# Where the operands of 6500 matrix products lie in SBUF: from an offset of 64 bytes to one of 128

## The chip, the cores and the metric

The kernel runs on 1 core of one Trainium2 chip. The metric is the device time of one execution in microseconds, as the median of several runs. One execution was also taken by the hardware profiler; all durations below come from that one.

## The reference, cut to what matters

Two layers of a diffusion backbone over 512 latent tokens of width 1024 with 256 context tokens. Layer 0 is attention (four global heads and four windowed heads with a sink), layer 1 a Fourier mixer over four channel groups. Each layer ends with a gated feed-forward part with a depthwise convolution of width 3. Everything is float32.

```python
y, yc = attention_mixers(h, hc, attn_w_in[a], ...)      # layer 0
y = fourier_mix(h) @ w_f                                # layer 1
x = x + g1 * rms_norm(y, norm_g[i, 1])
h = modulate(rms_norm(x, norm_g[i, 2]), sh2, sc2)
x = x + g2 * rms_norm(conv_ffn(h, ffn_w_up[i], ffn_conv_w[i], ffn_conv_b[i], ffn_w_down[i]), norm_g[i, 3])

def conv_ffn(h, w_up, conv_w, conv_b, w_down):          # D_FF = 2816
    u = h @ w_up
    ...                                                 # width-3 convolution along the tokens
    gate, val = jnp.split(u, 2, axis=-1)
    return (jax.nn.silu(gate) * val) @ w_down
```

## The kernel before

Activations are held transposed: channels on the 128 partitions, tokens along the row. Every large matrix product is done in fp32r; each operand is split into a high part and a rest (`split`: ScalarE copies to the high part, VectorE or GpSimd subtracts), and each product becomes three (`mm3`, lines 104 to 106): high weights by high data, high by rest, rest by high. `PE.matmul(out, lhsT=weights, rhs=moving)` loads 128 columns of `lhsT` into TensorE and streams `rhs` (256 to 512 columns) past them. So a product reads two places of SBUF, and the load of the weights of the next product (PEld in the profile) goes on while the moving operand of the present one streams. In names such as `mm<-hh,wl` the first name after the arrow is the moving operand and the second the weights.

The order of work: the modulation vectors and norms of the inputs; projections to keys and values, to queries; attention by head, with the remaining projections filled in between; the output projection; feed-forward of layer 0; Fourier mixing; feed-forward of layer 1; the last norm and the store. Weights arrive by DMA in three rotating `raw` buffers and are split into five rotating pairs `wh`/`wl`. Some weights are kept in the pairs `xh`/`xl` and `zh`/`zl`, which at other times hold activations as moving operands. In parts of the feed-forward stages, seven products of 256 columns take the place of eight (`seven_products`).

Where a tile lies follows from its pool: tiles of a pool follow one another in the order in which their tags first appear, each rounded up to 32 bytes, and a pool begins where the one below it ends. In the kernel before, counting modulo 256 bytes: `hh`, `hl` and `xT` start at 0, `wh` and `wl` at 192, `th`/`tl`, `kh`/`kl`, `B`, `Z` at 128, `qh`/`ql` at 192; the buffers of `xh`/`xl` and of `zh`/`zl` are partly at 0 and partly at 128, since some are 4224 bytes long, and weights kept in them are moved on by `SIDE` = 16 elements of 4 bytes (`beside`), to 64 or 192. So in nearly every product the two operands differ by 64 or by 192 modulo 256 bytes. Offsets inside a tile (the chunk `k`, the token block) are multiples of 256 bytes, except for rows of 288 elements (`A`, `ct`), which step by 128.

Of the kernel before, what the change touches and what calls it, by code (L numbers as in the profile page):

```python
# [10 lines left out]
F32 = mybir.dt.float32  # L11
F32R = mybir.dt.float32r
# [7 lines left out]
P = 128  # L20
D = 1024
KC = D // P
T = 512
TT = T // P
# [25 lines left out]
GP = [1, 1]  # L50
BP = [4, 1]

SIDE = 16

WARM = 36
HOT = [5, 8, 5, 6]
# [18 lines left out]
C_C, C_CC, C_MB, C_NG, C_CW, C_CB = 0, 8, 16, 112, 176, 440  # L75
C_SINK, C_ALL = 528, 532

K_ID, K_SEL, K_QD, K_ALL = 0, 128, 256, 260
# [3 lines left out]
def kernel(ctx: ExitStack, tc: tile.TileContext, a):  # L82
    nc = tc.nc
    V, S, G, PE, SY = nc.vector, nc.scalar, nc.gpsimd, nc.tensor, nc.sync
    cnt = [0]
    nbufs = {}

    def mk(pool, shape, dt=F32, tag=None, bufs=1):
        cnt[0] += 1
        n = nbufs.setdefault((id(pool), tag), (pool, bufs))[1]  # L90
        return pool.tile(shape, dt, tag=tag, name=f"{tag}_{cnt[0]}", bufs=n)
# [8 lines left out]
    def f(ap):  # L100
        return ap.bitcast(F32)
# [24 lines left out]
    def split(h, l, src, eng=V):  # L126
        i = S.copy(out=h, in_=src), eng.tensor_tensor(out=l, in0=src, in1=f(h), op=ALU.subtract)  # L127
        for j in i:
            held(j)

    cp = ctx.enter_context(tc.tile_pool(name="cp", bufs=1))
    wp = ctx.enter_context(tc.tile_pool(name="wp", bufs=1))
# [4 lines left out]
        return t  # L137

    def wpair(shape):
        return mk(wp, shape, F32R, "wh", 5), mk(wp, shape, F32R, "wl", 5)  # L140

    away = mk(ctx.enter_context(tc.tile_pool(name="dr", bufs=1, space=bass.MemoryType.DRAM)), [P, KC, T], F32, "away")
    cols = mk(cp, [P, C_ALL], F32, "cols")
    SY.dma_start(out=cols[:, :C_CW], in_=a["cols"][:, :C_CW])
    con = mk(cp, [P, K_ALL], F32, "con")
    xT = mk(cp, [P, KC, T], F32, "xT")
    yT = mk(cp, [P, KC, T], F32, "yT")
    hh = mk(cp, [P, KC, T], F32R, "hh")
    hl = mk(cp, [P, KC, T], F32R, "hl")
    ident = con[:, K_ID:K_ID + P]  # L150
    ones32 = mk(cp, [P, 32], F32, "ones32")
    V.memset(ones32, 1.0)
    scol = mk(cp, [P, 2, KC], F32, "scol")
    eps = mk(cp, [P, 1], F32, "eps")
    once = mk(cp, [P, 1], F32, "once")
    mk(cp, [P, 8], F32, "cpad")
    V.memset(eps, EPS)
    mods = mk(cp, [P, 2, 6, KC], F32, "mods")
    der = mk(cp, [P, 2, 4, KC], F32, "der")
# [16 lines left out]
    W4 = HT // 4  # L176
# [12 lines left out]

    def rstd(ps):  # L190
        w = ps.shape[1]
        v, t, r = (mk(cp, [P, W4], F32, "st_" + c, n)[:, :w] for c, n in (("v", 2), ("t", 1), ("r", 2)))
        S.activation(out=r, in_=ps, func=AF.Abs_reciprocal_sqrt, bias=eps, scale=1.0 / D)
        V.tensor_scalar(out=v, in0=ps, scalar1=1.0 / D, scalar2=EPS, op0=ALU.mult, op1=ALU.add)
        V.tensor_tensor(out=t, in0=r, in1=r, op=ALU.mult)
        V.scalar_tensor_tensor(out=t, in0=t, scalar=-0.5, in1=v, op0=ALU.mult, op1=ALU.mult)
        V.scalar_tensor_tensor(out=v, in0=t, scalar=1.5, in1=r, op0=ALU.add, op1=ALU.mult)
        return v
# [361 lines left out]
    with ExitStack() as es:  # L560
# [27 lines left out]
        with ExitStack() as e1:  # L588
# [21 lines left out]
            def load_kva(c):  # L610
                kva[c] = raw([P, 2, T], a["w_kva"][c])
# [4 lines left out]

            load_x(0)
            load_mod(0)
            SY.dma_start(out=con, in_=a["con"])
            load_kva(0)  # L620
            load_mod(1)
            SY.dma_start(out=cols[:, C_CW:], in_=a["cols"][:, C_CW:])
# [118 lines left out]
            for s in START.split():  # L741
                n = [int(c) for c in s[1:]]
# [163 lines left out]
        with ExitStack() as e2:  # L906
            at = e2.enter_context(tc.tile_pool(name="at", bufs=1, reuse_waits="tile"))
# [28 lines left out]
            def pv(head, Ps, vh, vl):  # L936
                is_a = head < 4
                po = mk(aps, [P, T], F32, "O", 1)
                cs, th, tl = {}, {}, {}

                def turn(kt):
                    t = kt - 2
                    lo, hi = (0, 4) if is_a or kt < 2 else (max(0, t - 1), min(4, t + 2))
                    c = cs[kt] = slice(lo * P, hi * P)
                    pt = mk(aps, [P, T], F32, "PT", 2)
                    for j in range(lo, hi):
                        if is_a:
                            off = kt * P
                        else:
                            off = kt * P if kt < 2 else TC + (t - max(0, j - 1)) * P  # L950
                        PE.transpose(out=pt[:, j * P:(j + 1) * P], in_=Ps[j][:, off:off + P], identity=ident)  # L951
                    th[kt] = mk(at, [P, T], F32R, "th", 2)
                    tl[kt] = mk(at, [P, T], F32R, "tl", 2)
                    split(th[kt][:, c], tl[kt][:, c], pt[:, c])

                turn(0)
                turn(1)
                yield
                for kt in range(6):
                    c = cs[kt]  # L960
                    mm3(po[:, c], vh[:, kt, :], vl[:, kt, :], th[kt][:, c], tl[kt][:, c], kt == 0, kt == 5)
                    if kt < 4:
                        turn(kt + 2)
                    if kt < 5:
                        yield
                if head < KEPT:
                    S.copy(out=kept(head)[0], in_=po.rearrange("p (t d) -> p t d", d=P))
                else:
                    split(hh[:, head, :], hl[:, head, :], po)
                yield  # L970

            V.tensor_scalar(out=nsink, in0=cols[:, C_SINK:C_SINK + 4], scalar1=-1.0, scalar2=None, op0=ALU.mult)
            pend = iter(())

            def queries_t(head):
                qh = mk(at, [P, T], F32R, "qh", 1)
# [10 lines left out]
            for head in range(8):  # L987
# [6 lines left out]
                for j in range(TT):  # L994
# [4 lines left out]
                    if is_a:  # L999
                        for i in range(2):  # L1000
                            o = ps[:, 128 + i * 384:128 + (i + 1) * 384]
                            mm3(o, qh[:, qs], ql[:, qs], kh[:, i * 384:(i + 1) * 384],
                                kl[:, i * 384:(i + 1) * 384], True, True)
                        reg, n = ps[:, 128:896], NK
                    else:
# [4 lines left out]
                        o = ps[:, 512:512 + nl]  # L1010
# [7 lines left out]
                        reg, n = ps[:, 256:512 + nl], TC + nl  # L1018
# [30 lines left out]
                    i = 4 * (head - 6) + j  # L1049
# [41 lines left out]

    def beside(pool, shape, tag):
        n, m = shape[1:]
        return mk(pool, [P, 2 * SIDE + n * m], F32R, tag, 4)[:, SIDE:SIDE + n * m].rearrange("p (a b) -> p a b", b=m)

    class Pairs:
        def __init__(self, es):
# [14 lines left out]
            return [beside(self.first, shape, n) for n in ("xh", "xl")]  # L1112

        def spare_weights(self, shape):
            return [beside(self.pool, shape, n) for n in ("zh", "zl")]

    def up_weights(l, pairs, fis, eng=V):
        for fi in fis:
# [342 lines left out]
    with ExitStack() as es:  # L1461
        up = es.enter_context(tc.tile_pool(name="up", bufs=1, reuse_waits="tile", side="right"))
        M1 = 258
        B = [mk(up, [P, 4, 256], F32R, "B%d" % i) for i in range(2)]
        A = [mk(up, [P, 4, 288], F32R, "A%d" % i)[:, :, :M1] for i in range(2)]
        N = [mk(up, [4, M1 + 30], F32R, "N%d" % i)[:, :M1] for i in range(2)]
        mk(up, [P, 24], F32, "upad")
        wk = es.enter_context(tc.tile_pool(name="wk", bufs=1, reuse_waits="tile", side="right"))
        zs = ExitStack()
        zp = zs.enter_context(tc.tile_pool(name="zp", bufs=1, reuse_waits="tile"))  # L1470
        ft = wpair([P, 2, 256])
        st = wpair([P, TT, 256])
        Z = [mk(zp, [P, TT, 4, 256], F32R, "Z%d" % i) for i in range(2)]
        ct = [mk(zp, [P, 32 + TT * 288], F32R, "ct%d" % i)[:, SIDE:SIDE + TT * 288].rearrange(
            "p (t m) -> p t m", t=TT)[:, :, :M1] for i in range(2)]
        split(ft[0], ft[1], raw([P, 2, 256], a["dft_c"]), G)
        lc = raw([P, TT, M1], a["dft_lc"])
        ls = raw([P, TT, 256], a["dft_ls"])
# [2 lines left out]
        def over_channels(g, h):  # L1481
# [11 lines left out]
            if h:  # L1493
                split(Z[0][:, 2:4, g, :], Z[1][:, 2:4, g, :], ps)
                return
            for t in range(2):
                rc = r0[:, 2 * t:2 * t + 1]
                held(S.activation(out=Z[0][:, t, g, :], in_=ps[:, t, :], func=AF.Copy, scale=rc))
                held(V.scalar_tensor_tensor(out=Z[1][:, t, g, :], in0=ps[:, t, :], scalar=rc,
                                            in1=f(Z[0][:, t, g, :]), op0=ALU.mult, op1=ALU.subtract))  # L1500

# [53 lines left out]
        def group(g, ts):  # L1555
            cosines(g, [v[:, g, :] for v in A], [z[:, :, g, 0:P] for z in Z], ts, fb[:, g:g + 1])
            ps = over_tokens((g // 2,), g % 2, [z[:, :, g, P:] for z in Z], st, ts, g % 2 == 1)
            if ts[-1] == TT - 1 and g % 2:
# [51 lines left out]
        group(1, [2, 3])  # L1610
        cosines(None, N, [z[:, :, :, P] for z in Z], list(range(TT)), fb[:4, 4:5])
        group(3, [2, 3])
# [5 lines left out]
        for d in range(KC):  # L1618
            wh, wl = w_f.pop() if w_f else fourier_weights(d)
# [7 lines left out]
            pp = mk(pps, [P, T], F32, "mm", 6)  # L1627
            mm3(pp[:, :M1], nyh[:, d * P:(d + 1) * P], nyl[:, d * P:(d + 1) * P], N[0], N[1], True, False)
            for g in range(4):
                mm3(pp[:, :M1], wh[:, 0, g, :], wl[:, 0, g, :], A[0][:, g, :], A[1][:, g, :], False, g == 3)  # L1630
            qs = mk(wk, [P, 256], F32, "qs", 2)
# [14 lines left out]
    with ExitStack() as es:  # L1646
# [13 lines left out]
        for k in range(0, KC, 2):  # L1660
            t = mk(cp, [P, T], F32, "sq", 2).rearrange("p (a b) -> p a b", a=2)
# [97 lines left out]
```

## Time and profile before

| | |
|---|---|
| median of 3 runs | 1138.37 us (1137.33 to 1138.49) |
| the profiled execution | 1137.78 us |
| its span | 1136.0 us, 19565 instructions |
| mean granted clock of TensorE | 0.996 |
| HBM read, written | 148.28 MB, 6.29 MB |

In rows of groups, a line reads: source line, engine, operation, out<-in, rows by columns of the array in use, shape of the output, count, then busy us, mean ns of one, and idle time of the engine before it. Matmuls are pipelined: a product's duration reaches past the start of the next one, so durations overlap and their sum is more than the time. In rows for one tile or one line, three numbers with slashes are the smallest, the median and the largest duration in ns, and after them stand the first and the last start.

### The profile page before, as it was taken

How to read it: one execution, taken by the hardware profiler on the slowest of the kernel's cores; microseconds unless marked ns; L12 is line 12 of the kernel's file. 1: busy time of each engine (PE TensorE's matmuls, PEld its weight loads, DVE VectorE, ACT ScalarE, POOL GpSimd, SP SyncE). 2: the span in 40 equal slices, each digit the busy share in tenths (PEclk: the TensorE clock that was granted, in tenths of full speed). 3: DMA queues.
4: the chain of work that ended last, by engine and by line, in shares of the span. 5: the costliest groups of instructions: out<-in, count | busy, mean ns of one | idle time of the engine just before them, and what ended most of it. 6: DMA issues, size and time to landing. Idle time of an engine off the chain costs nothing.

```text
span 1136.0 us, 19565 instructions
## 1 busy us (share of the span) xinstructions
PE 1105.1 (97%) x7810; PEld 962.1 (85%) x7810; DVE 902.3 (79%) x1469; ACT 595.4 (52%) x1068; POOL 174.6 (15%) x180
## 2 busy tenths in 40 slices
PE   9999999999999999999999999999999999999995
PEld 5689888868888978987899898779888898999995
DVE  4678777765679976987999668978998998879755
ACT  4342356666666633552465445557746555555533
POOL 1136332421420000000000143620000000000012
PEclk9999999999999999999999999999999999999998
DMA  9676101075143355635535401742215533322342
GB/s 370 252 237 217 44 1 39 10 266 207 38 186 112 103 200 217 223 121 204 196 111 173 135 2 57 231 122 113 74 47 163 189 103 116 103 91 93 105 144 75
DMA packets 33763, 155.83 MB, mean 137 GB/s; under 512 B 3460, under 2 KB 8196, under 8 KB 22024
## 3 DMA queue, kind: packets, MB, share of 16 engines
q1 hardware_dynamic: 32520, 150.39, 37.5%
q0 software_dynamic: 1152, 4.19, 1.6%
q8 instruction: 61, 1.00, 0.4%
q14 instruction: 30, 0.25, 0.1%
HBM read 148.28 MB, written 6.29 MB: 136 GB/s over the span
## 4 chain that ended last, share of the span: by engine, by line
PE 77%; DVE 14%; ACT 5%; DMA 2%; issue 2%; POOL 1%; DVEq 0%; POOLq 0%; ACTq 0%; SPq 0%
PE mm L104 21%; PE mm L106 20%; PE mm L105 20%; DVE wl L127 2%; PE PT L951 1%; DMA raw<-in_w_up 1%; DVE md_t L305 1%; PE O L104 1%; PE O L105 1%; PE gm L530 1%; PE gm L104 1%; PE gm L106 1%; ACT wh L127 1%; PE gm L105 1%; PE O L106 1%
## 5 line engine op out<-in xcount | busy, mean ns | idle before, releaser
L127 ACT CAST wh<-raw 128x1024 fp32r<-128x1024 f32 (+2 forms) x207 | 190.6, 933 | 167.8 <-PE mm L105 115.4
L127 DVE TENSOR_TENSOR wl<-raw,wh 128x1024 fp32r<-128x1024 f32 (+2 forms) x197 | 214.7, 1098 | 52.2 <-ACT wh L127 51.9
L104 PE MATMUL mm<-hh,wh 128*128 128x256 f32 (+1 forms) x632 | 204.8, 325 | 1.9 <-ACT yT L926 0.9
L106 PE MATMUL mm<-hh,wl 128*128 128x256 f32 (+1 forms) x632 | 202.0, 320 | 0.4 <-DVE wl L127 0.2
L105 PE MATMUL mm<-hl,wh 128*128 128x256 f32 (+1 forms) x632 | 202.0, 320 | 0.0
L280 POOL TENSOR_TENSOR gacc<-gacc,sq 128x256 f32<-128x256 f32 (+1 forms) x33 | 28.0, 848 | 712.6 <-ACT sq L278 711.9
L104 PEld LDWEIGHTS mm<-hh,wh 128*128 128x128 f32 x632 | 118.7, 188 | 17.0 <-ACT sq L1206 4.6
L105 PEld LDWEIGHTS mm<-hl,wh 128*128 128x128 f32 x632 | 118.7, 188 | 10.3
L106 PEld LDWEIGHTS mm<-hh,wl 128*128 128x128 f32 x632 | 118.7, 188 | 10.2 <-DVE wl L127 1.2
L104 PE MATMUL mm<-zh,wh 128*128 128x256 f32 x384 | 109.5, 285 | 1.2 <-ACT sq L1209 0.6
L104 PE MATMUL mm<-xh,wh 128*128 128x512 f32 (+1 forms) x302 | 107.1, 355 | 0.0
L105 PE MATMUL mm<-zl,wh 128*128 128x256 f32 x384 | 107.1, 279 | 0.0
L106 PE MATMUL mm<-zh,wl 128*128 128x256 f32 x384 | 107.0, 279 | 0.0
L105 PE MATMUL mm<-xl,wh 128*128 128x512 f32 (+1 forms) x302 | 106.5, 353 | 0.0
L106 PE MATMUL mm<-xh,wl 128*128 128x512 f32 (+1 forms) x302 | 106.2, 352 | 0.0
L104 PEld LDWEIGHTS mm<-zh,wh 128*128 128x128 f32 x384 | 72.1, 188 | 5.5 <-ACT sq L1209 4.2
L106 PEld LDWEIGHTS mm<-zh,wl 128*128 128x128 f32 x384 | 72.5, 189 | 0.0
L105 PEld LDWEIGHTS mm<-zl,wh 128*128 128x128 f32 x384 | 72.1, 188 | 0.0
L104 PEld LDWEIGHTS mm<-xh,wh 128*128 128x128 f32 x302 | 56.7, 188 | 9.4 <-issue 1.6
L105 PEld LDWEIGHTS mm<-xl,wh 128*128 128x128 f32 x302 | 56.7, 188 | 8.5 <-issue 0.4
L106 PEld LDWEIGHTS mm<-xh,wl 128*128 128x128 f32 x302 | 56.8, 188 | 8.0
L1267 ACT ACTIVATE cv<-mm,cols 128x512 f32<-128x512 f32 x59 | 45.7, 776 | 23.1 <-PE mm L106 17.4
(435 smaller groups left out, 2796.1 us busy)
## 6 DMA issues: line engine op xcount, KB each, us to landing
raw<-in_w_up SPq DMA_DIRECT2D x42, 1024.0 KB, 4.9
xT<-in_mod_r SPq DMA_DIRECT2D x20, 1024.0 KB, 5.0
raw<-in_w_down SPq DMA_DIRECT2D x32, 384.0 KB, 3.1
raw<-in_mod_p SPq DMA_DIRECT2D x8, 1024.0 KB, 4.9
raw<-in_w_down SPq DMA_DIRECT2D x16, 512.0 KB, 3.9
raw<-in_w_in SPq DMA_DIRECT2D x6, 1024.0 KB, 8.2
yT<-in_mod_r SPq DMA_DIRECT2D x10, 512.0 KB, 7.3
raw<-in_w_out SPq DMA_DIRECT2D x4, 1024.0 KB, 5.1
```

Source lines behind the costliest of these rows:

```text
L104: i = PE.matmul(out, lhsT=ah, rhs=bh, start=start, stop=False, skip_group_check=skip)
L105: PE.matmul(out, lhsT=ah, rhs=bl, start=False, stop=False, skip_group_check=skip)
L106: return i, PE.matmul(out, lhsT=al, rhs=bh, start=False, stop=stop, skip_group_check=skip)
L127: i = S.copy(out=h, in_=src), eng.tensor_tensor(out=l, in0=src, in1=f(h), op=ALU.subtract)
L280: G.tensor_tensor(out=self.acc[:, sl], in0=self.acc[:, sl], in1=sq[:, sl], op=ALU.add)
L305: m = V.scalar_tensor_tensor(out=t, in0=yT[:, k, hs], scalar=der[:, l, gi, k:k + 1], in1=R, op0=ALU.mult, op1=ALU.mult)
L530: PE.matmul(ps[32 * q:32 * q + 32, :], lhsT=spad[:, k, :], rhs=w[:, q * T:(q + 1) * T], start=k == 0, stop=k == KC - 1)
L951: PE.transpose(out=pt[:, j * P:(j + 1) * P], in_=Ps[j][:, off:off + P], identity=ident)
L1267: S.activation(out=cv, in_=ps, func=AF.Identity, bias=bc, scale=wc[1])
```

## The change

The places of tiles are shifted with unused pieces, so that the moving operand of nearly every fp32r product starts at 0 modulo 256 bytes and its weights at 128, or the reverse. For that, `SIDE` becomes 32 elements, the buffers `xh`/`xl` get 1088 elements (4352 bytes, a multiple of 256) when they hold weights, `zh`/`zl` 1024, `A` and `ct` rows of 320 elements, and unused tiles stand ahead of `wh`, behind `wl`, and ahead of `qh`, `th`, `Z` and `ct` and behind `N`. To make room, `scol` takes the place of the columns of `cols` from which it is computed, `eps` and `once` become two more columns of `con`, and `st_r` has one buffer, not two.

```diff
-SIDE = 16
+SIDE = 32
+XW = 1088
+QPAD, TPAD, ZPAD, UPAD = 16, 48, 64, 56
+WPAD = 24
...
     def wpair(shape):
-        return mk(wp, shape, F32R, "wh", 5), mk(wp, shape, F32R, "wl", 5)
+        if (id(wp), "wh") in nbufs:
+            return mk(wp, shape, F32R, "wh", 5), mk(wp, shape, F32R, "wl", 5)
+        mk(wp, [P, WPAD], F32, "wpad")
+        w = mk(wp, shape, F32R, "wh", 5), mk(wp, shape, F32R, "wl", 5)
+        mk(wp, [P, 48], F32, "wpad2")
+        return w
...
-    con = mk(cp, [P, K_ALL], F32, "con")
+    con = mk(cp, [P, K_ALL + 2], F32, "con")
...
-    scol = mk(cp, [P, 2, KC], F32, "scol")
-    eps = mk(cp, [P, 1], F32, "eps")
-    once = mk(cp, [P, 1], F32, "once")
-    mk(cp, [P, 8], F32, "cpad")
+    scol = cols[:, C_C:C_C + 16].rearrange("p (a b) -> p a b", a=2)
+    eps = con[:, K_ALL:K_ALL + 1]
+    once = con[:, K_ALL + 1:K_ALL + 2]
...
-        v, t, r = (mk(cp, [P, W4], F32, "st_" + c, n)[:, :w] for c, n in (("v", 2), ("t", 1), ("r", 2)))
+        v, t, r = (mk(cp, [P, W4], F32, "st_" + c, n)[:, :w] for c, n in (("v", 2), ("t", 1), ("r", 1)))
...
-            SY.dma_start(out=con, in_=a["con"])
+            SY.dma_start(out=con[:, :K_ALL], in_=a["con"])
...
+                    if (id(at), "th") not in nbufs:
+                        mk(at, [P, TPAD], F32, "tpad")
                     th[kt] = mk(at, [P, T], F32R, "th", 2)
...
+            mk(at, [P, QPAD], F32, "qpad")
...
     def beside(pool, shape, tag):
         n, m = shape[1:]
-        return mk(pool, [P, 2 * SIDE + n * m], F32R, tag, 4)[:, SIDE:SIDE + n * m].rearrange("p (a b) -> p a b", b=m)
+        return mk(pool, [P, XW], F32R, tag, 4)[:, SIDE:SIDE + n * m].rearrange("p (a b) -> p a b", b=m)
...
         def spare_weights(self, shape):
-            return [beside(self.pool, shape, n) for n in ("zh", "zl")]
+            n, m = shape[1:]
+            o = SIDE if n * m + SIDE <= 1024 else 0
+            return [mk(self.pool, [P, 1024], F32R, t, 4)[:, o:o + n * m].rearrange("p (a b) -> p a b", b=m)
+                    for t in ("zh", "zl")]
...
-        A = [mk(up, [P, 4, 288], F32R, "A%d" % i)[:, :, :M1] for i in range(2)]
-        N = [mk(up, [4, M1 + 30], F32R, "N%d" % i)[:, :M1] for i in range(2)]
-        mk(up, [P, 24], F32, "upad")
+        A = [mk(up, [P, 4, 320], F32R, "A%d" % i)[:, :, :M1] for i in range(2)]
+        N = [mk(up, [4, 320], F32R, "N%d" % i)[:, :M1] for i in range(2)]
+        mk(up, [P, UPAD], F32, "upad")
...
+        mk(zp, [P, ZPAD], F32, "zpad")
         Z = [mk(zp, [P, TT, 4, 256], F32R, "Z%d" % i) for i in range(2)]
-        ct = [mk(zp, [P, 32 + TT * 288], F32R, "ct%d" % i)[:, SIDE:SIDE + TT * 288].rearrange(
-            "p (t m) -> p t m", t=TT)[:, :, :M1] for i in range(2)]
+        mk(zp, [P, 32], F32, "zpad2")
+        ct = [mk(zp, [P, TT, 320], F32R, "ct%d" % i)[:, :, :M1] for i in range(2)]
```

More of the change, by code (lines that the diff above doesn't have):

```diff
@@ L148 @@
     hh = mk(cp, [P, KC, T], F32R, "hh")
+    ident = con[:, K_ID:K_ID + P]
     hl = mk(cp, [P, KC, T], F32R, "hl")
-    ident = con[:, K_ID:K_ID + P]
     ones32 = mk(cp, [P, 32], F32, "ones32")
     V.memset(ones32, 1.0)
-    scol = mk(cp, [P, 2, KC], F32, "scol")
-    eps = mk(cp, [P, 1], F32, "eps")
-    once = mk(cp, [P, 1], F32, "once")
-    mk(cp, [P, 8], F32, "cpad")
+    scol = cols[:, C_C:C_C + 16].rearrange("p (a b) -> p a b", a=2)
+    eps = con[:, K_ALL:K_ALL + 1]
+    once = con[:, K_ALL + 1:K_ALL + 2]
     V.memset(eps, EPS)
```

## The prediction

> **What bounds the kernel now.** I read the page's totals first, then the chain that ended last, then the busy times by stage, and only then the products by shape.
>
> ```profile
> span 1136.0 us, 19565 instructions
> PE 1105.1 (97%) x7810; PEld 962.1 (85%) x7810; DVE 902.3 (79%) x1469; ACT 595.4 (52%) x1068; POOL 174.6 (15%) x180
> PEclk9999999999999999999999999999999999999998
> PE 77%; DVE 14%; ACT 5%; DMA 2%; issue 2%; POOL 1%; DVEq 0%; POOLq 0%; ACTq 0%; SPq 0%
> ```
>
> ```profile
> 340.00:680.00 340.00, 338.57 (x2108) 297.57 (x2107) 283.50 (x361) 166.97 (x255) 15.06 (x18) 1.00 0.43 150
> 770.00:1106.00 336.00, 333.70 (x2208) 298.38 (x2207) 287.11 (x420) 193.10 (x315) 4.29 (x6) 1.00 0.33 111
> ```
>
> TensorE is busy for 97% of the span and carries 77% of the chain. The second view has two stretches, most of the two feed-forward parts (length, then PE, PEld, DVE, ACT and POOL busy, granted clock, DMA). There TensorE is idle for 1.43 and 2.30 us out of 676, at a granted clock of 1.00, while VectorE, next in line, is busy for 83% and 85%. So in these stages a nanosecond per product goes straight into the time, and the question is one number: how long one fp32r product holds TensorE, and whether the place of its operands changes that.
>
> **Does place matter at all?** First groups by shape in two short windows (the last two columns are mean ns and idle time), then starts from the timeline of the same stage, then a 512-column run.
>
> ```profile
> L104 PE MATMUL mm<-zh,wh 128*128 128x256 f32 x2 | 0.6, 276 | 0.0
> ```
>
> ```profile
> L104 PE MATMUL mm<-zh,wh 128*128 128x256 f32 x3 | 0.8, 280 | 0.0
> L106 PE MATMUL mm<-zh,wl 128*128 128x256 f32 x3 | 0.8, 279 | 0.0
> ```
>
> ```profile
> 500.28 0.28 PE L104 MATMUL mm<-zh,wh 128*128 128x256 f32 x1
> 501.19 0.28 PE L106 MATMUL mm<-zh,wl 128*128 128x256 f32 x1
> 502.48 0.28 PE L104 MATMUL mm<-zh,wh 128*128 128x256 f32 x1
> 503.42 0.28 PE L106 MATMUL mm<-zh,wl 128*128 128x256 f32 x1
> ```
>
> ```profile
> L106 PE MATMUL mm<-hh,wl 128*128 128x512 f32 x7 | 2.8, 394 | 0.0
> L104 PE MATMUL mm<-hh,wh 128*128 128x512 f32 x6 | 2.3, 388 | 0.0
> ```
>
> The first row is from 500.7 to 501.1 us, the next two from 502.5 to 503.3. Helper, shape and weights pool are the same; the moving buffer differs. From the tile sizes in the code, wh and wl sit at 192 modulo 256 bytes. The zh buffer of the first window sits at 128 (moving minus weights: -64), that of the second at 0 (+64). Eight intervals between starts take 0.91 us in the first (114 ns each) and 0.94 in the second (118). That is the same 4 ns by which the durations differ, so a duration can be read as the interval plus a constant. The two signs of the 64-byte offset do not cost the same: quick is 276, slow is 280. With 512 columns, at +64, the products of a triple go from 388 to 394, though all have the same offset: place is not the only thing that sets the step.
>
> One row speaks against place:
>
> ```profile
> L106 PE MATMUL mm<-ct,Z 128*4 128x258 f32 x4 | 1.1, 282 | 0.0
> ```
>
> These products load 4 columns of weights, not 128, so that almost no weight load lies beside them, and with two columns more than 256 they still take 282 ns. The slow step exists without a rival stream.
>
> [...]
>
> **The change, part by part.** By adding up the tile sizes, afterwards hh, hl, xT, the gated pairs xh/xl, the blocks zh/zl, A, B, N, Z, th/tl, kh/kl and ch/cl start at 0 modulo 256, and wh/wl, ct, qh/ql and the weights kept in xh/xl at 128. No compute instruction and no transfer is added or removed. The effect is in the product rate, on these groups:
>
> ```profile
> L105 PE MATMUL mm<-hl,wh 128*128 128x256 f32 x400 | 112.1, 280 | 0.0
> L105 PE MATMUL mm<-zl,wh 128*128 128x256 f32 x384 | 107.1, 279 | 0.0
> L105 PE MATMUL mm<-hl,xh 128*128 128x256 f32 x128 | 36.3, 284 | 0.0
> L106 PE MATMUL mm<-xh,wl 128*128 128x256 f32 x112 | 31.3, 279 | 0.0
> L105 PE MATMUL mm<-wl,hh 128*128 128x256 f32 x112 | 31.4, 280 | 0.0
> L106 PE MATMUL gm<-wh,hl 128*128 128x256 f32 x96 | 26.9, 280 | 0.0
> L105 PE MATMUL mm<-xl,zh 128*128 128x256 f32 x84 | 23.5, 280 | 0.0
> L105 PE MATMUL mm<-hl,wh 128*128 128x512 f32 x224 | 87.6, 391 | 0.0
> L106 PE MATMUL mm<-hh,wl 128*128 128x512 f32 x224 | 88.0, 393 | 0.1
> L105 PE MATMUL mm<-xl,wh 128*128 128x512 f32 x190 | 74.7, 393 | 0.0
> L106 PE MATMUL mm<-xh,wl 128*128 128x512 f32 x190 | 74.9, 394 | 0.0
> L104 PE MATMUL mm<-xh,wh 128*128 128x512 f32 x190 | 75.4, 397 | 0.0
> L105 PE MATMUL mm<-xT,wh 128*128 128x512 f32 x64 | 25.0, 390 | 0.0
> ```
>
> ```profile
> L105 PE MATMUL mm<-hl,xh x160: 276/276/470, 277.2 to 789.7; 128*128 128x256 f32 x128, 128*128 128x258 f32 x32
> ```
>
> Each group runs on three lines (L104 to L106) with the same count; I take the line with the fewest waits. The mean of 284 for hl,xh holds waits; its median in the last row is 276.
>
> The good end: every product becomes quick. With 256 columns the excess over 276 is 4 ns x 400 + 3 x 384 + 0 x 128 + 3 x 112 + 4 x 112 + 4 x 96 + 4 x 84 = 4256 ns for one line, 12.8 us for three. With 512 columns, over 388, L105 gives 3 x 224 + 5 x 190 + 2 x 64 = 1750 ns, which I use for L104 too, and L106 gives 5 x 224 + 6 x 190 + 2 x 64 = 2388; together 5.9 us. Sum 18.7 us. The feed-forward stages hold 4316 products (2108 + 2208), against 3 x 1794 = 5382 in the list: about three quarters, where all of it counts. Of the last quarter, in stages where the chain passes through other engines, I count half: 18.7 x 0.875 = 16.4 us.
>
> The bad end: every product becomes slow. With 256 columns up to 280: (1 x 384 + 4 x 128 + 1 x 112) x 3 = 3.0 us. With 512 columns up to 397, the highest group mean here: L105 gives 6 x 224 + 4 x 190 + 7 x 64 = 2552 ns, taken twice, L106 4 x 224 + 3 x 190 + 7 x 64 = 1914; together 7.0 us. Sum 10.0 us, of which I let all count. A step beyond what is seen, 4 ns more on 3 x 1316 products of 256 columns, would add 15.8 us more; that is left to the tail.
>
> Where between the ends? No product of before runs steadily at 128. But now and then an odd one does, where the weights loaded during it belong to another kind of product. th (at 128) is followed in places by a product with weights from hh (at 0):
>
> ```profile
> L106 PE MATMUL O<-th,wl 128*128 128x512 f32 x32 | 12.6, 395 | 0.0
> ```
>
> ```profile
> L106 PE MATMUL O<-th,wl x1: 390/390/390, 158.5 to 158.5; 128*128 128x512 f32 x1
> L106 PE MATMUL O<-th,wl x1: 390/390/390, 188.1 to 188.1; 128*128 128x512 f32 x1
> L104 PE MATMUL O<-th,wh x1: 397/397/397, 162.9 to 162.9; 128*128 128x512 f32 x1
> ```
>
> The first two are the first and last I looked up of eight on L106, at 390 to 392; the last row is one of three on L104, all at 397. Against the group mean of 395 and the quick step of 388, the eight at 390 are (395 - 390) / 7 = 0.7 of the way to the good end; all eleven, with a mean of 392.1, are 0.4 of the way. It is thin, since such a product stands alone and its neighbours set its phase, but these are the nearest rows. I take 0.55, between the two: 0.55 x 16.4 = 9.0 us.
>
> The other edits. One buffer for st_r, not two, lets a root on ScalarE wait until VectorE has read the last one; eps, once and scol become columns of con and cols; raw moves to 32 modulo 256.
>
> ```profile
> L193 ACT ACTIVATE st_r<-misc,eps x11: 245/313/315, 289.7 to 1108.9; 128x64 f32<-128x64 f32 x9, 128x4 f32<-128x4 f32 x2
> L633 ACT ACTIVATE scol<-cols x1: 215/215/215, 2.8 to 2.8; 128x16 f32<-128x16 f32 x1
> L157 DVE MEMSET eps<- x1: 59/59/59, 0.8 to 0.8; 128x1 f32 x1
> ```
>
> The roots lie far apart (eleven in 819 us, five more in the first 778), so the lost buffer costs nothing; without that distance each would wait at most for its own length, 16 x 0.31 = 5 us. eps is set at 0.8 us, long before a root reads it, and scol is computed at 2.8 us from the columns it now overwrites. All zero. One exception to the offset: the weights of the last down-projection group of layer 0 that go into zh/zl fill their tile and stay at 0, like their moving operand: 3 x 8 x 2 x 3 = 144 products, at 4 ns 0.6 us either way.
>
> Sum: the profiled execution took 1137.78 us (span 1136.0 and 1.78 around it; 0.59 under the median of 1138.37), less 9.0 gives 1128.8 us.
>
> **The rivals.**
> [...]
> - 128 holds the products in the slow step. At +64 the 256-column products are slow and at -64 quick, so an offset is not good merely because it is not zero, and 128 lies as near to one as to the other. It decides once the 256-column groups average 280 and the 512-column ones above 393. Price 10.0 us, time 1147.8 us, slower. Against it: the 390s; for it: the 397s.
> - Half of the products gain: TensorE gets quicker, but VectorE's 83 to 85% leaves less room and the weight pairs that it makes come late, above all in attention. I have put half of the last quarter down for it; if half of the 9.0 us is lost, 1133.3 us, still faster.
>
> **How the numbers follow.** 0.2% (2.3 us) is about what a measurement of this kernel can tell from no change. Faster, with or without the half lost: 0.54. No difference: 0.17. Slow step: 0.29. The likeliest is 1128.8 us, its own range 1119 (the good end, with the groups not listed) to 1134. The range for 8 in 10 reaches on the slow side to 1148, the bad end (about 0.1 of the chance lies beyond, in the step not seen), and on the quick side to 1113, a little past the good end (1137.8 - 16.4 = 1121.4) for the groups not listed and for a step quicker than any seen.
>
> **What would show it.** Right: zh,wh and hl,wh with 256 columns at 276 to 277, 512-column groups at 388 to 390, PE busy in both feed-forward windows shorter by the same microseconds, PE still idle for under 1%. [...] Rival two: medians at 280 where -64 gave 276 (hl,xh, half of zh), 512 columns at 395 or more. Wrong in another way: a 256-column step below 276 or above 282, which no row of before has as a steady value; or ScalarE's roots waiting for VectorE.

## The result and the profile after

The change makes the kernel slower: 1148.63 us (median of 6 runs, 1146.91 to 1149.85) against 1137.85 us beside it; the ratio is 1.0094, 95% interval 1.0082 to 1.0106. The profiled execution took 1147.2 us, 9.4 more than the 1137.78 of before. Predicted were 1128.8 us; the forecast had the wrong sign, and the time is that of the rival that holds the products in the slow step (1147.8 us).

The page of the kernel after: its totals, the granted clock by slice and the chain that ended last.

```profile
span 1145.4 us, 19566 instructions
PE 1117.0 (98%) x7810; PEld 972.4 (85%) x7810; DVE 903.1 (79%) x1469; ACT 595.8 (52%) x1068; POOL 174.8 (15%) x180
PEclk9999999999999999999999999999999999999998
PE 86%; DVE 9%; ACT 2%; issue 1%; DMA 1%; POOL 0%; SPq 0%; DVEq 0%; POOLq 0%; ACTq 0%
```

The same number of matrix products keeps TensorE busy for 11.9 us more (1105.1 to 1117.0), the clock is the same, and the other engines are as before to within 1 us. TensorE's share of the chain rises from 77% to 86%, while VectorE's falls from 14% to 9% and ScalarE's from 5% to 2%: with slower products, TensorE waits less for them. Next, the two feed-forward stretches, in the columns of the prediction.

```profile
340.00:680.00 340.00, 338.86 (x2077) 296.82 (x2077) 280.40 (x355) 165.75 (x251) 11.50 (x13) 1.00 0.42 150
770.00:1106.00 336.00, 334.50 (x2174) 298.01 (x2174) 288.21 (x426) 191.46 (x315) 0.74 (x1) 1.00 0.33 113
```

At full clock, 2077 and 2174 products fit where 2108 and 2208 did. The groups by shape (mean ns in the last column but one) show which; the helper's lines are L107 to L109 now.

```profile
L108 PE MATMUL mm<-hl,wh 128*128 128x256 f32 x400 | 113.0, 282 | 0.0
L108 PE MATMUL mm<-zl,wh 128*128 128x256 f32 x384 | 108.1, 282 | 0.0
L108 PE MATMUL mm<-hl,xh 128*128 128x256 f32 x128 | 36.9, 288 | 0.0
L108 PE MATMUL mm<-wl,hh 128*128 128x256 f32 x112 | 31.9, 285 | 0.0
L108 PE MATMUL mm<-hl,wh 128*128 128x512 f32 x224 | 88.4, 395 | 0.0
L109 PE MATMUL mm<-hh,wl 128*128 128x512 f32 x224 | 88.5, 395 | 0.1
L108 PE MATMUL mm<-xl,wh 128*128 128x512 f32 x190 | 75.1, 395 | 0.0
```

```profile
L108 PE MATMUL mm<-hl,xh x160: 277/282/467, 278.3 to 795.9; 128*128 128x256 f32 x128, 128*128 128x258 f32 x32
```

Each group is slower, with 256 columns by 2 to 5 ns and with 512 by 2 to 4, and none has waits to show for it. For hl,xh, where a pair of 64 bytes had given a median of 276, it is 282.

A finer measure is the interval from a product's start to the start of the next, worked out from the trace's starts for the fp32r products of 256 and 512 columns with no gap between them (intervals up to 130 and 250 ns), and sorted by offset (moving operand minus the weights loaded during it, modulo 256; 64 is +64, 192 is -64):

| columns, offset | before: count, mean ns | after: count, mean ns |
|---|---|---|
| 256, +64 | 1934, 117.1 | |
| 256, -64 | 2111, 115.7 | |
| 256, 128 | | 3915, 118.9 |
| 256, 0 | 31, 114.7 | 175, 120.1 |
| 512, +64 | 1186, 229.3 | |
| 512, -64 | 419, 232.6 | |
| 512, 128 | 11, 230.5 | 1607, 232.6 |
| 512, 0 | | 11, 231.7 |

The products at offset 0 before, and eleven each in the two last rows, are odd ones; the others at 0 after are mostly the 144 that the prediction names as its exception. With 256 columns the difference is 1934 x 1.8 + 2111 x 3.2 = 10.2 us, with 512 columns 1186 x 3.3 = 3.9 us: 14.1 us. All fp32r products with the gaps behind them went from 1026.0 to 1036.3 us, 10.3 more. So about 4 us of the longer intervals went into gaps that had been there anyway.

### The profile page after: what moved, and what is told of

Same layout as the page of the kernel before. It is cut to its first block, busy times and chain, and to the rows that moved or that the text cites. A ratio compares the mean times of both kernels' runs of the same rounds, so it can differ in the third digit from the quotient of the medians.

```text
span 1145.4 us, 19566 instructions
## 1 busy us (share of the span) xinstructions
PE 1117.0 (98%) x7810; PEld 972.4 (85%) x7810; DVE 903.1 (79%) x1469; ACT 595.8 (52%) x1068; POOL 174.8 (15%) x180
## 4 chain that ended last, share of the span: by engine, by line
PE 86%; DVE 9%; ACT 2%; issue 1%; DMA 1%; POOL 0%; SPq 0%; DVEq 0%; POOLq 0%; ACTq 0%
PE mm L107 25%; PE mm L108 24%; PE mm L109 23%; PE PT L958 1%; DVE wl L130 1%; DVE md_t L312 1%; PE O L107 1%; PE gm L537 1%; PE O L108 1%; PE gm L107 1%; PE gm L109 1%; PE gm L108 1%; PE O L109 1%; DMA raw<-in_w_kva 1%; DVE md_t L245 1%
## 5 line engine op out<-in xcount | busy, mean ns | idle before, releaser
L107 PE MATMUL mm<-hh,wh 128*128 128x256 f32 (+1 forms) x632 | 206.5, 327 | 1.9 <-ACT yT L933 0.9
L109 PE MATMUL mm<-hh,wl 128*128 128x256 f32 (+1 forms) x632 | 203.4, 322 | 0.1
L107 PEld LDWEIGHTS mm<-hh,wh 128*128 128x128 f32 x632 | 119.0, 188 | 17.0 <-ACT sq L1220 3.7
L109 PEld LDWEIGHTS mm<-hh,wl 128*128 128x128 f32 x632 | 119.0, 188 | 10.3 <-DVE wl L130 0.3
L107 PE MATMUL mm<-zh,wh 128*128 128x256 f32 x384 | 110.6, 288 | 0.6 <-ACT sq L1218 0.6
L109 PE MATMUL mm<-zh,wl 128*128 128x256 f32 x384 | 108.4, 282 | 0.0
L107 PE MATMUL mm<-xh,wh 128*128 128x512 f32 (+1 forms) x302 | 107.9, 357 | 0.0
L109 PE MATMUL mm<-xh,wl 128*128 128x512 f32 (+1 forms) x302 | 106.6, 353 | 0.0
L107 PEld LDWEIGHTS mm<-zh,wh 128*128 128x128 f32 x384 | 72.3, 188 | 4.8 <-ACT sq L1223 3.5
L109 PEld LDWEIGHTS mm<-zh,wl 128*128 128x128 f32 x384 | 72.3, 188 | 0.0
L107 PEld LDWEIGHTS mm<-xh,wh 128*128 128x128 f32 x302 | 56.9, 188 | 9.8 <-issue 1.6
L109 PEld LDWEIGHTS mm<-xh,wl 128*128 128x128 f32 x302 | 56.9, 188 | 8.4
```

Of the source, the lines that this page charges most:

```text
L107: i = PE.matmul(out, lhsT=ah, rhs=bh, start=start, stop=False, skip_group_check=skip)
L109: return i, PE.matmul(out, lhsT=al, rhs=bh, start=False, stop=stop, skip_group_check=skip)
```

## The experiments

**Is it the place, or the edits that made room for it?** The kernel before, with all edits but the places:

```diff
+    scol = cols[:, C_C:C_C + 16].rearrange("p (a b) -> p a b", a=2)
+    eps = con[:, K_ALL:K_ALL + 1]
+    once = con[:, K_ALL + 1:K_ALL + 2]
+    mk(cp, [P, 40], F32, "cpad")          # keeps what follows at its old place
...
-    v, t, r = (... for c, n in (("v", 2), ("t", 1), ("r", 2)))
+    v, t, r = (... for c, n in (("v", 2), ("t", 1), ("r", 1)))
```

> The kernel before with only the other edits (one buffer for st_r, scol in cols, eps and once in con) and unused pieces so that every tile stays where it was. Theory one (places make the loss): no change, 1136.5 to 1139.5 us, ratio within 0.2% of 1. Theory two (the other edits make it): 1145 to 1150 us.

1137.49 us, ratio 0.9998 (0.9985 to 1.0012). The other edits cost nothing, as the prediction had it.

**Only the weights moved by 64 bytes, either way.** The kernel after with its weights at 192 or at 64 modulo 256 instead of 128; all else stays.

```diff
-SIDE = 32
+SIDE = 48            # the other kernel: 16
-WPAD = 24
+WPAD = 40            # the other kernel: 8
-        mk(wp, [P, 48], F32, "wpad2")
+        mk(wp, [P, 72 - WPAD], F32, "wpad2")
```

> The changed kernel with one place moved: wh/wl, and the weights kept in xh/xl and zh/zl, at 192 modulo 256 instead of 128; all moving operands stay at 0. So 3324 of the 256-column products and 1578 of the 512-column ones are at +64, and those where wh/wl is the moving operand (816 and 144) at -64. Theory one, with the steady steps of the kernel before (+64: 117.1 and 229.3 ns, -64: 115.7 and 232.6): about 0.8 ns more per 256-column product and 0.6 less per 512-column one than before, 1140 us, that is 8 us of the loss given back. Theory two (the loss is not in the relation of the operands): 1148 us as the changed kernel.

> The changed kernel with wh/wl, and the weights kept in xh/xl and zh/zl, at 64 modulo 256 instead of 128: the mirror of the run before, 3324 of the 256-column products and 1578 of the 512-column ones at -64. Theory one: 256-column products near 115.7 ns (duration 278), 512-column ones near 232.6 (395), about 1140 us. Theory two: 1148 us. A third theory, that only the distance counts and not its sign, would make this run and the one before equal row by row.

Weights at 192: 1137.7 us, ratio to before 0.9999 (0.9985 to 1.0012). Weights at 64: 1138.76 us, ratio 1.0002 (0.9989 to 1.0015). Either shift of 64 bytes gives back the whole loss, with the padding, the pitches and the long buffers still in place. The groups of the first:

```profile
L108 PE MATMUL mm<-hl,wh 128*128 128x256 f32 x400 | 112.1, 280 | 0.0
L108 PE MATMUL mm<-zl,wh 128*128 128x256 f32 x384 | 107.2, 279 | 0.0
L109 PE MATMUL mm<-hh,wl 128*128 128x512 f32 x224 | 88.2, 394 | 0.1
```

and of the second:

```profile
L108 PE MATMUL mm<-hl,wh 128*128 128x256 f32 x400 | 111.3, 278 | 0.0
L108 PE MATMUL mm<-zl,wh 128*128 128x256 f32 x384 | 106.2, 277 | 0.0
L109 PE MATMUL mm<-hh,wl 128*128 128x512 f32 x224 | 88.7, 396 | 0.0
```

The times are equal, the products are not. By intervals, mostly +64 (weights at 192) gives 117.2 ns with 256 columns and 229.2 with 512; mostly -64 (weights at 64) gives 114.3 and 233.2. The two column counts want different offsets.

**The bare products.** Weights at 0, 16, ... 240, moving operand at 0, and the same with fewer columns of weights:

```python
for o in OFFS:                       # 0, 16, ... 240
    run(o, 256, 4)                   # 4 groups of 24 products of 256 columns
    run(o, 512, 2)
for m in (4, 32, 64):                # columns of weights
    for o in (64, 128):
        run(o, 256, 2, m); run(o, 512, 1, m)
```

> This kernel leaves out the whole model: it copies x to the output and runs only triples of fp32r products, with hh/hl at 0 modulo 256 bytes and the weights W0, W16, ... W240 at that many bytes modulo 256, with 256 and with 512 columns, and at the end with 4, 32 and 64 columns of weights instead of 128. Theory one (the step is set by moving minus weights, modulo 256, with nothing else of the kernel): W192 (+64) about 118 ns per 256-column product and 229 per 512-column one, W64 (-64) 113 to 116 and 232 to 233, W128 about 119 and 232 to 233, W0 about 120 and 232; the spread over all sixteen places some 5 to 7 ns. Theory two (the slow-down of the changed kernel comes from the other edits, or from other engines on the same memory): all sixteen places within 1 ns of each other. With 4 columns of weights: if two reading streams collide, the step is the quick one (113 and 226) wherever the weights lie; if the moving stream makes the steps alone, it stays at 118 to 120.

Intervals inside a group with 256 columns: 120.0 ns at 0, 117.8 at -64 (weights at 64), 118.7 at 128, 117.8 at +64 (weights at 192), and between 116.6 and 120.1 for all sixteen. With 512: 226.8 at 0, 233.3 at -64, 232.4 at 128, 229.1 at +64. So the best place for 512 columns is no offset at all (I had expected about 232 there), and the expected 113 to 116 ns at -64 did not appear: the same offset was at 114.3 in the kernel above. With fewer columns of weights (each row mixes the runs at -64 and at 128):

```profile
L121 PE MATMUL n<-hl,W 128*4 128x256 f32 x32 | 8.9, 277 | 0.0
L121 PE MATMUL n<-hl,W 128*32 128x256 f32 x32 | 8.8, 276 | 0.0
L121 PE MATMUL n<-hl,W 128*4 128x512 f32 x16 | 6.3, 396 | 0.0
```

By intervals, the 256-column products at 128 take 113.6 ns with 4 columns of weights and 113.5 with 32, against 118.7 with 128; with 64 columns they take 116.7. So at 128 a product of 256 columns is slow because of the load beside it. At -64 they take 116.7, 113.3 and 118.9 ns with 4, 32 and 64 columns. The 512-column products, 396 in the row above and 391 to 395 on the other two lines, start every 231 to 232 ns with 4 columns, little under the 232.4 and 233.3 of the full load. The load of weights is part of the matter, not all of it. Offset 0 was not run with fewer columns.

**Absolute place, and single odd products.** A second sweep, with a second moving pair gh/gl at 128, weights wA to wH at 0, 32, ... 224, and, in a run at +64 (wG), every eighth weight tile taken from wO, at 128:

```python
wh, wl = w[odd if odd and k == 4 else tag]
```

> Again only triples of fp32r products, the model left out, x copied to the output. Weights wA to wH lie at 0, 32, ... 224 modulo 256 bytes; high and low parts are now 5120 bytes apart (4608 in the first sweep). hh/hl lie at 0, gh/gl at 128, zh/zl at 0 with chunks 1024 bytes apart (hh: 2048). Theory one, relation alone: gh with wA equals hh with wE (128), gh with wG equals hh with wC (-64), gh with wC equals hh with wG (+64), each within 1 ns in mean duration; hh,wE 281 to 282 with 256 columns, 394 to 395 with 512; hh,wA 282 and 389. If the distance of high and low weights matters too, hh,wC with 256 columns goes from 280 in the first sweep to 276 to 277, as in the run with the weights at 64. wO: one triple in eight at 128 inside a run at +64 (wG). If an odd product tells the steady step, n<-hh,wO is 281 to 282 and 394 to 395, as wE; if it takes its neighbours' step instead, 279 to 280 and 391. wP: wC with a 384-column product ahead of each 24; if the state a run starts in lasts, its mean differs from wC by over 1 ns, else not.

```profile
L133 PE MATMUL n<-hh,wC 128*128 128x256 f32 x32 | 8.8, 276 | 0.0
L133 PE MATMUL n<-gh,wG 128*128 128x256 f32 x32 | 8.8, 276 | 0.0
L133 PE MATMUL n<-hh,wG 128*128 128x256 f32 x60 | 16.8, 279 | 0.0
L133 PE MATMUL n<-gh,wC 128*128 128x256 f32 x32 | 8.9, 279 | 0.0
L133 PE MATMUL n<-hh,wE 128*128 128x256 f32 x32 | 9.0, 281 | 0.0
L133 PE MATMUL n<-hh,wE 128*128 128x512 f32 x16 | 6.3, 395 | 0.0
L133 PE MATMUL n<-hh,wO 128*128 128x512 f32 x2 | 0.8, 392 | 0.0
```

```profile
L133 PE MATMUL n<-hh,wO x6: 276/281/392, 322.6 to 340.7; 128*128 128x256 f32 x4, 128*128 128x512 f32 x2
L134 PE MATMUL n<-hl,wO x6: 281/287/398, 322.7 to 341.0; 128*128 128x256 f32 x4, 128*128 128x512 f32 x2
```

Rows one and two are -64 from two absolute places, rows three and four +64: there the difference counts, not the place. At 128 the agreement is looser than I had expected: hh with wE is at 281 on all three lines, gh with wA at 281, 284 and 285. The steady runs at 128 (wE) stand at 281 and 395. The odd products at 128 lie anywhere from 276 to 287 with 256 columns and up to 398 with 512; those of 512 columns average 392 on L133 and 394 on L134, against 395 in the steady run. A single one tells nothing of the steady step. (From start to start, three of the four pairs of 256 columns take 116 or 117 ns on one line and 123 or 124 on the other: only the two together come near the steady 119.) Offset -64 is at 276 here and at 281 or so in the first sweep, and within this sweep it is at 276 with hh, but at 278 when a product of 384 columns stands ahead of each group (wP) and at 281 with zh:

```profile
L133 PE MATMUL n<-zh,wC 128*128 128x256 f32 x32 | 9.0, 281 | 0.0
```

Why one offset has several values is still open here.

**Places by use.** Since 512 columns want 0 and 256 columns -64, each weight tile is placed by what will read it (to make room, some small tiles move into shared ones):

```diff
-    def wpair(shape):
+    def wpair(shape, o=QUICK):                 # QUICK = 16 elements: 64 bytes
...
+    def wpair512(shape):                       # for products of 512 columns
+        return wpair(shape, 0)
```

> A version that takes the places from the runs so far: weights of 512-column products at the same place as their moving operand modulo 256 (offset 0), those of 256-column products so that moving minus weights is -64, by moving each pair inside a larger buffer; all else as in the changed kernel (552 of the 256-column products, with weights in xh/xl and a few more, stay at offset 0). Relation theory: 256 columns at -64 take 114.3 ns per start (before: 116.4 on average), about 3600 dense ones, 7.6 us less; some 530 at offset 0 take 120, 1.9 us more; 512 columns at offset 0 take 226.7 (before: 230.2), about 1610 dense ones, 5.6 us less: 11 us together, 1126 us. Rival: the 512-column step at offset 0 held only in the bare sweep (eleven odd ones inside the model took 232 at 0): then about 6 to 3 us less, 1131 to 1135 us. Rival two, places only matter through 128: 1137 us.

1132.29 us, ratio to before 0.9954 (0.9939 to 0.9969): faster than both kernels, though not the 1126 us expected. The products account for it, against the intervals of before: 2.5 us from 256 columns at -64, 4.0 us from 512 columns, less 1.6 us for the 256-column products left at 0 (119.5 ns), together 4.9 of the 5.2 us gained.

```profile
L108 PE MATMUL mm<-hl,wh 128*128 128x256 f32 x400 | 111.8, 279 | 0.0
L108 PE MATMUL mm<-zl,wh 128*128 128x256 f32 x384 | 106.7, 278 | 0.0
L108 PE MATMUL mm<-hl,wh 128*128 128x512 f32 x224 | 87.3, 390 | 0.0
```

The 512-column products do what the sweep promised: 390 ns, and 227.7 from start to start. Those of 256 columns at -64 take 115.7 ns on average, not 114.3. Two stretches of this trace, 936.1 to 939.3 us and 940.0 to 942.3 us, with the same helper, shape and offset, show two steps:

```profile
L108 PE MATMUL mm<-zl,wh 128*128 128x256 f32 x5 | 1.4, 281 | 0.0
```

```profile
L107 PE MATMUL mm<-hh,wh 128*128 128x256 f32 x4 | 1.1, 276 | 0.0
L108 PE MATMUL mm<-zl,wh 128*128 128x256 f32 x3 | 0.8, 276 | 0.0
```

The products run at 118 ns from start to start, then at 113 to 114, with a short gap between (intervals of 272 and 221 ns). Two causes seemed possible: the distance between the high and the low weights of a pair (256 modulo 1024 bytes here, 0 in the kernel with weights at 64), or what ran before.

**The distance.** Both weights of a pair in one tile, 4096 bytes apart:

```diff
+        both = mk(wp, [shape[0], WW], F32R, "w", 5)      # WW = 2112
-            v = mk(wp, [shape[0], WW], F32R, t, 5)[:, o:o + n]
+            v = both[:, o + i * D:o + i * D + n]
```

> As the kernel placed by use, but the high and low weights of a pair lie in one tile, 4096 bytes apart (0 modulo 1024); there they are 21760 bytes apart (256 modulo 1024). The operands' difference modulo 256 is the same in both: 0 for 512 columns, -64 for 256 columns. Theory of the distance (what matters beside the difference modulo 256 is the distance between the two weights of a pair modulo 1024, 0 being the quick one): the 256-column products at -64 start every 113.5 to 114.5 ns instead of 115.7, the groups hl,wh and zl,wh fall from 279 and 278 to 277 or 276, and the time is about 5 us under 1132.3, 1126 to 1128. Rival (the step that a run of products falls into is set by what ran before it, not by the distance): 115 to 116 ns, 1131 to 1133 us. In both, 512 columns at 0 stay at 227 to 228 ns.

The theory of the distance falls: 115.7 ns again. And the time is 1137.87 us, ratio to before 1.0011 (0.9999 to 1.0022), so the gain is gone for a reason that neither theory had. The longest of TensorE's waits in that stage, then the windows around it (length, PE, PEld, DVE, ACT, POOL busy, granted clock):

```profile
PE mm L109 <- DVE w L130: 3.5, 1, 3.5
```

```profile
835.00:840.00 5.00, 5.00 (x23) 4.13 (x22) 5.00 (x6) 3.45 (x5) 0.00 (x0) 1.00 0.00 0
840.00:845.00 5.00, 1.54 (x8) 1.13 (x6) 5.00 (x7) 1.30 (x2) 0.00 (x0) 0.89 0.00 0
845.00:850.00 5.00, 4.96 (x12) 3.90 (x13) 5.00 (x7) 1.67 (x2) 0.00 (x0) 0.50 0.20 54
850.00:855.00 5.00, 5.00 (x22) 4.09 (x21) 3.61 (x5) 2.76 (x3) 0.00 (x0) 0.93 0.08 9
```

VectorE, at 5.00 of 5.00 us, is late with one weight tile, and TensorE stands for 3.5 us, from 841.5 to 845.0 us. The clock falls to 0.50 at 843.9 us, inside the wait, and stays there for 6.8 us (the 0.89 and 0.93 are the windows in which it falls and rises): twelve 512-column products start every 427 ns instead of 227.

Set product by product beside the trace of the kernel placed by use, TensorE falls 5.6 us behind in this wait and the slow clock after it, and makes up 1.4 us of that by 943 us. Earlier it loses 1.2 us at about 200 us and 1.3 us at about 720 us, where the clock is at 0.50 for 3.4 us. That is most of the 7.2 us between these two executions (1139.29 and 1132.08 us); the other runs of this kernel have no trace.

The clock fell inside the wait of 3.5 us, 2.3 us after the last product's end; but the fall at about 720 us had no gap of more than 0.62 us in TensorE's work shortly before it, so a long wait alone does not explain these falls. Why VectorE was late only here, whether for the shared tile or by a narrow margin, was not settled; it is nearly as busy in the kernel placed by use, at 4.97 us in the window from 840 to 845 us, where TensorE is busy for 4.81.

**What ran before.** Bare products again. First, five pairs (wA to wE, 4096 to 5120 bytes apart), all at -64, behind a group at 128 (tile n) and behind 512 columns at 0 (tile m):

```python
for tag, far in FAR:
    run("pre", tag, far, 128, 256, 1)
    run("n", tag, far, 64, 256, 3)
    run("pre", tag, far, 0, 512, 1)
    run("m", tag, far, 64, 256, 3)
    run("z", tag, far, 0, 512, 2)
```

> The model is left out: only runs of fp32r products, with the moving operand at 0 modulo 256 and five pairs of weights that lie 4096, 4352, 4608, 4864 and 5120 bytes apart (wA to wE). Each pair is used at an offset of -64 with 256 columns twice: behind a group at 128 (tile n) and behind a group of 512 columns at 0 (tile m). Then two groups of 512 columns at 0 (tile z). Theory of the distance: n and m agree for each pair; wA and wE (0 modulo 1024) at 276 ns, wC (512 modulo 1024) at 279 to 280, wB and wD between or at either. Rival (set by what ran before): n and m of one pair differ by 2 ns or more, and the pairs do not order by distance. Tile z: 388 to 390 ns for all if only the difference of the operands counts with 512 columns.

```profile
L118 PE MATMUL m<-hl,wC 128*128 128x256 f32 x24 | 6.7, 281 | 0.0
L118 PE MATMUL m<-hl,wA 128*128 128x256 f32 x24 | 6.7, 281 | 0.0
L118 PE MATMUL n<-hl,wC 128*128 128x256 f32 x24 | 6.6, 276 | 0.0
L118 PE MATMUL n<-hl,wA 128*128 128x256 f32 x24 | 6.6, 276 | 0.0
```

On this line all five pairs gave 276 in n and 281 in m. Same weights, same offset, same shape: what ran before decides in these runs, and the distance does not. Then each of four offsets behind eight predecessors:

```python
for q, o in (("m", 64), ("p", 192), ("h", 128), ("z", 0)):
    run("pre", 128, 256, 1); run(q + "a", o, 256, 2)
    run("pre", 0, 512, 1);   run(q + "b", o, 256, 2)
    run("pre", 128, 512, 1); run(q + "c", o, 256, 2)
    ...
```

> The model is left out: runs of 48 fp32r products of 256 columns at each of four offsets (tiles m: -64, p: +64, h: 128, z: 0; weights of a pair 4352 bytes apart), each behind eight different things (second letter): a, 24 products of 256 columns at 128; b, 24 of 512 columns at 0; c, 24 of 512 at 128; d, 24 of 512 at -64; e to i, 24 of 512 at 0 and then: e, one product of 512 columns at -64; f, one of 256 at 128; g, one of 64 columns; i, two of 64 columns. Theory of two states (at +64 and -64 a run of products stays in the step it falls into, 113 to 114 ns or 118 ns from start to start, and what ran before decides which; 128 and 0 have no quick one): ma shows 276 ns and mb 281; among the p rows both 276 and 281 appear; all h rows are at 281 to 284 and all z rows at 282 to 283, whatever ran before. Rival (128 has a quick state too, and the model only happened to enter the slow one): some h row is at 276 to 278. Second rival (the step belongs to the offset, and the runs before differed for another reason): all m rows agree, and all p rows.

```profile
L117 PE MATMUL hb<-hh,wb 128*128 128x256 f32 x16 | 4.6, 285 | 0.0
L117 PE MATMUL zb<-hh,wb 128*128 128x256 f32 x16 | 4.5, 283 | 0.0
L117 PE MATMUL mb<-hh,wb 128*128 128x256 f32 x16 | 4.5, 281 | 0.0
L117 PE MATMUL hc<-hh,wb 128*128 128x256 f32 x16 | 4.5, 281 | 0.0
L117 PE MATMUL pb<-hh,wb 128*128 128x256 f32 x16 | 4.5, 280 | 0.0
L117 PE MATMUL mc<-hh,wb 128*128 128x256 f32 x16 | 4.4, 276 | 0.0
L117 PE MATMUL pc<-hh,wb 128*128 128x256 f32 x16 | 4.4, 276 | 0.0
```

At -64 six of the eight predecessors lead to 276 and two (b and g) to 281; at +64 one (c) leads to 276 and seven to 279 or 280. At 128 all eight stay at 281 to 285 on this line, at 0 all at 283. So both signs of a 64-byte offset have two steps, 113 to 114 and 118 ns from start to start, and a run of 48 keeps its step to the end; 128 has only slow ones, 120 ns in b and f and 118.5 to 118.7 in the other six. One extra product is enough to tip it: behind 512 columns at 0, a single product of 256 columns at 128 (f) turns 281 into 276. The predecessor is not all: behind 512 columns at -64 (d) this sweep has 276, but the row of zh above, behind the same kind of product, had 281; there the chunks of the moving operand lie 1024 bytes apart instead of 2048 and the two weights 5120 instead of 4352, and no run separates these. What in TensorE or SBUF makes two steps was not found.

The model shows the same. Of all stretches of six successive 256-column products, 54% at -64 and 22% at +64 average 115.5 ns or less in the kernel before, and none of 3078 at 128 in the kernel after. In the kernel with weights at 64, where 256-column products at -64 run in a program whose 512-column products are at -64 too (as in d), 86% of the stretches at -64 do.

**Steering it.** In the kernel placed by use, the first pair of weights of a 256-column stretch goes to 128, so that the rest runs behind products at 128; run beside the kernel placed by use.

```diff
+        first = o == QUICK and lasto[0] == 0
+        lasto[0] = o
+        o = FIRSTO if first else o             # FIRSTO = 32 elements: 128 bytes
```

> As the kernel placed by use, but the first pair of weights of a 256-column stretch that follows 512-column products lies at 128 instead of 64 modulo 256; it serves 360 products, and about 21 stretches at -64 in the feed-forward blocks then begin behind products at 128. Theory of two states (behind products at 128 a stretch at -64 falls into the quick step; behind 512 columns at 0, into the slow one): the first products of those stretches, some 15 to 20 each at 118 ns, go to 113 to 114; the mean of all at -64 falls from 115.7 to 114.7 to 115.2, the 360 at 128 take 118 to 119 as they did before, and the time is 1 to 3 us under the kernel placed by use. Rival (in the model something else sets the state): the mean at -64 stays at 115.7 and the time is the same within 1 us.

> The kernel placed by use once more, beside the one with the first pair at 128, on the same chip: 1131 to 1134 us by every theory, 256 columns at -64 at 115.7 and 512 columns at 0 at 227 to 228 ns.

1134.77 us, ratio to before 0.9963 (0.9951 to 0.9975), against 1134.56 us and 0.9964 (0.9952 to 0.9976) for the kernel placed by use: no difference. The trace shows both parts of a stretch, first at 128, then at -64, 910.9 to 912.0 us and 912.6 to 916 us:

```profile
L108 PE MATMUL mm<-hl,wh 128*128 128x256 f32 x4 | 1.1, 284 | 0.0
```

```profile
L108 PE MATMUL mm<-zl,wh 128*128 128x256 f32 x6 | 1.7, 276 | 0.0
```

The steering works in part: quick stretches at -64 rise from 52% to 65%, and the mean at -64 falls from 115.7 to 115.2 ns. But the products at 128 take 120.0, not the 118 to 119 I expected, and the sum is the same: 3203 x 115.2 + 341 x 120.0 = 409.9 us against 3543 x 115.7 = 409.9. The sweep had shown that price, and I had overlooked it: a run at 128 behind 512 columns at 0 (hb) takes 120.1 ns. In both of these traces the clock is also granted at 0.50 near 715 us, for 10.2 and 6.8 us (the 8 in the row below, from the kernel with the first pair at 128), again with no gap of more than 0.61 us shortly before:

```profile
PEclk9999999999999999999999999899999999999998
```

The first trace of the kernel placed by use has no such stretch. Half of its length, 5.1 and 3.4 us, is my estimate of what it costs. The kernel placed by use stays the best that was run.

## Why the prediction was wrong, point by point

- **TensorE is the bound, and a nanosecond per product counts: right**, though not in full. 14.1 us of longer intervals became 10.3 us in the stretches of fp32r products, since gaps of about 4 us were filled, and 9.4 us of time.
- **Place matters: right.** Weights moved by 64 bytes give back 10.9 us (1148.63 to 1137.7). For the products of 256 columns at 128 the load of the next weights has a part in it: they take 113.6 ns with 4 columns of weights loaded beside them and 118.7 with 128. The row of 4-column products, which I set against place, shows less than I read from it: a load of 4 columns is not almost nothing, it takes 85 to 87 ns in the trace of before (711.4 to 713.0 us), against 188 with 128 columns.
- **"Quick is 276 at -64, slow is 280 at +64": the reading failed.** The two zh windows showed two steps that either offset can have, and I took them for the mark of the offset. In the bare runs what ran before decides; in the kernel before, -64 is quick more often (54% of stretches against 22%).
- **The share of 0.55 towards the good end: the step that failed.** It came from eleven odd products at 128, read as if they told the steady step, and it made a gain of 9.0 us. But odd products at 128 lie between 276 and 287 with 256 columns while the steady run is at 281, and with 512 their 392 and 394 stand beside a steady 395. The steady value was the bad end, with nothing of the good one: no stretch of 256 columns at 128 was quick (0 of 3078), 512 columns took 232.6 ns, and in place of the gain the intervals grew by 14.1 us.
- **The bad end, 10.0 us: right in sum, wrong in its parts.** I had 3.0 us from 256 columns (a step of up to 280) and 7.0 from 512 (up to 397), all counted. Measured were 10.2 and 3.9 us, of which two thirds counted. The steps at 128 reach 281 to 285, beyond the 280 that I took as the highest; I had left that to the tail. The 512-column groups stand at 395, but for xh,wh on the first line of the helper, 397 before and 399 after. That the rival's 1147.8 us lies within 1 us of the measured time is luck: three errors cancel.
- **What would show it:** for the slow step, rival two, I named medians at 280 where -64 gave 276, and 512 columns at 395 or more. The rows above have 282 and 395. The group wl,hh, at 285, also goes beyond the 282 that I had named as the limit for a 256-column step.
- **The other edits at zero: right**, by the kernel with those edits alone.
- **Half of a gain lost to VectorE:** not tried by the change itself, since nothing got quicker. The trace of the kernel with the pairs in one tile lost most of its gain at a wait of 3.5 us for VectorE and in the slow clock after it (5.6 us together), but why VectorE was late there stayed open.

## What to carry to other kernels

Before placing operands by an offset, measure a steady run of the very shape at that offset, of some dozens of products and behind the predecessors that it will have; a single odd product in a trace tells nothing. If a group's durations fall into two values at one offset, look at what ran before, not only at where the operands lie. Where TensorE is the bound and VectorE nearly so, look at the longest wait and at the granted clock before you credit or blame the products: here one late weight tile cost 5.6 us, as much as the best placing had gained.

## What the runs showed of the hardware that was not expected

- fp32r products of 256 columns with operands 64 bytes apart modulo 256 have two lasting steps, 113 to 114 ns and 118 ns from start to start; at 128 and at 0, with 128 columns of weights, only 118 to 120 ns were seen in steady runs. A run of 48 stays in its step to the end; one other product ahead of it can tip it (281 to 276 ns), and in the model the step was seen to change at a short gap (intervals of 272 and 221 ns).
- With only 4 or 32 columns of weights loaded beside them, the same products at 128 take 113 to 114 ns.
- Products of 512 columns take 226.8 to 227.7 ns in runs at offset 0, about 229 at +64 and 232.3 to 233.3 at -64 and 128, while 256 columns average 114.3 to 115.7 at -64 in the traces of the model, 117.1 to 117.2 at +64, and take 119 to 120 at 0. At -64 and 128 the 512-column step is still 231 to 232 with only 4 columns of weights loaded beside them.
- A single wait of 3.5 us cost 5.6 us, because the granted clock was at 0.50 for 6.8 us in and after it (twelve 512-column products started every 427 ns instead of 227). In four traces (this one, the two runs of steering and the one with weights at 64) the clock also fell to 0.50 for 3.4 to 10.2 us near 720 us with no gap of more than 0.62 us shortly before; why was not found.
